# Attention on one core: the fourth product of weights and V by seven smaller ones in 21 periods instead of 6, joint VectorE operations, and instruction orders written out anew

## The chip, the cores and the metric

One core of a Trainium2 chip runs the whole kernel; seven other cores are idle. The metric is the device time of one execution in microseconds (us), median of several runs. Five engines work side by side, each through its own list of instructions in order: TensorE (PE in the profile; its weight loads are PEld), VectorE (DVE), ScalarE (ACT), GpSimd (POOL) and SyncE (SP), of which the last issues transfers only. An instruction that needs another engine's result waits on a semaphore, and everything behind it on its engine waits too.

## The reference

Softmax attention over 8 batches of 2048 rows with 512 columns, without a mask:

```python
def reference(q, k, v):                       # each (8, 2048, 512), float32
    d_k = q.shape[-1]
    scores = np.matmul(q, k.transpose(0, 2, 1)) / np.sqrt(d_k)
    attn_weights = special.softmax(scores, axis=-1).astype(np.float32)
    return np.matmul(attn_weights, v)
```

Q, K and V are rounded to float16 as they are loaded; products accumulate in float32.

## The kernel before, in words

**Seven products for eight.** A product of two matrices that are cut into 2x2 blocks takes eight products of blocks. The kernel uses a scheme with seven, numbered 1 to 7, and pays for it with sums of blocks: four sums of the left matrix's blocks, four of the right's (`s1`, `s2`, `s4`, a third that is written in place, and `t1`, `t2`, `t4`, `t3`), and additions of results. Results add up in PSUM where two products go to the same bank, and through a copy or an addition where they don't.

**Scores.** K (transposed) times Q is done in groups (`Group`, L336 on): a group makes a 256 x 1024 piece of the scores in 14 matmuls of 512 columns. After each product one instruction moves its result on: `after1` copies bank x to bank y, `after5` and `after6` copy to a scratch tile `cz`, `after7` and `after3` add to it, `after4` and `after2` take exponentials straight from the banks, and `exp_right` takes one of 1024 elements from `cz`. The exponentials are the weights, in float16, in four block tiles: `left[0]`, `left[1]` and two in `right`.

**Periods.** The work is cut into 32 periods (`NP`; four per batch, `qt` is a period's number within its batch). A period `g` does four score groups for later weights and finishes 512 rows of the output from weights that are ready: two pairs of blocks of 128 rows, `a` and `b`, each by seven products with V's blocks (`Pair.product`, L484), of which each is 8 matmuls of 256 columns.

**Inner products.** Products 1, 2 and 5 of `a` and `b` together (called x, y and z) are again a 2x2 product of blocks, and are done by seven smaller products each: `fine` (L688 on), 28 matmuls of 128 columns instead of 16 of 256 for the two. Its parts 1 to 4 are words `s1` to `s4` for x, `t` for y, `u` for z and `r` for w; w is product 4 of both. Which are done so is `INNERS`, by `qt`, and `INNERS_AT` for single periods: x, y, z nearly everywhere, w in the third period of a batch except the first (periods 6, 10, 14, 18, 22, 26). An inner product needs a copy of 256 columns from bank to bank (L733), two copies of 128 to a scratch tile `ci` (L736, L741), and two additions of 128 columns from it (L742 for a, L746 for b). `a_sums` (L663) makes its sums of weights, `vi_sums` (L271) those of V; the sums for x and y are joined in one instruction of 1024 elements where `s` is 4.

**Output.** The row sums of the weights come out as one more column of products 3 and 5. `rate` (L521) takes a reciprocal for each block, `scaled` (L493, ScalarE) scales a result out of its bank, `final` (L496, VectorE) scales and adds, and a few results are added on GpSimd (L613, which takes the second part from weights' space that is free by then) or on VectorE (L583). `store` (L506) issues each 128 x 256 piece on SP.

**What sets the order.** The lists of instructions are set by hand, not by a scheduler (`manual_schedule`). Each period has 28 slots, one for each score product in a fixed order (`QORDER`), plus 6. Tables say after which slot each product of weights and V (`PRODUCTS`, `ENDS`), each sum (`SUMS`, `SUMS_AT`) and each load or transposition for the next batch (`PLAN`) is issued. The evictions follow their product at once. Loads go through POOL's queue, transpositions (DMA) and stores through SP's. PSUM's eight banks are five pools: `qx` two, `qy` and `qz` one each, for scores; `px` and `pz` two each, for the output. The opening (batch 0, first weights) is a list of words of its own (`OPENING`), with whole score tiles (`t40x` and the like, L311) in `qx`, after quarters (L327) with exponentials of 256 elements.

Of the kernel before, what the change touches and what calls it, by code (L numbers as in the profile page):

```python
# [12 lines left out]
def kernel(  # L13
# [7 lines left out]

# [41 lines left out]
    INNERS = ("xyz", "xyz", "xyzw", "xyz")  # L63
    INNERS_AT = {0: "", 2: "xyz", NP - 2: "xz", NP - 1: "xyz"}
    ALL = True
# [3 lines left out]
    stage = ctx.enter_context(tc.tile_pool(name="stage", bufs=2))  # L69
    ppool = ctx.enter_context(tc.tile_pool(name="ppool", bufs=2))  # L70
    spool = ctx.enter_context(tc.tile_pool(name="spool", bufs=1))
    opool = ctx.enter_context(tc.tile_pool(name="opool", bufs=8))
    czpool = ctx.enter_context(tc.tile_pool(name="czpool", bufs=2))
    ipool = ctx.enter_context(tc.tile_pool(name="ipool", bufs=1))
    psum = {}
    for name, bufs in (("qx", 2), ("qy", 1), ("qz", 1), ("px", 2), ("pz", 2)):
        psum[name] = ctx.enter_context(
            tc.tile_pool(name="ps_" + name, bufs=bufs, space=bass.MemoryType.PSUM)
        )

    def bank(name):
        name = "pz" if name == "py" else name
        t = psum[name].tile([P, 512], F32, tag=name)
        return t
# [3 lines left out]
    ident32 = ipool.tile([P, P], F32, tag="t2", name="ident32")  # L88
    ident_dram = nc.inline_tensor(np.eye(P, dtype=np.float32), name="attn_identity")
    nc.scalar.dma_start(out=ident32[:], in_=ident_dram.ap())  # L90
    ident = ipool.tile([P, P], F16, tag="t4", name="ident")

    ksum = [const.tile([P, NCH, 2, 2, P], F16, name=f"ks{n}") for n in (1, 2, 4)]
    kops = []
    for c in range(NCH):
        raw = const.tile([P, CH, ND, P], F16, name=f"kraw{c}")
        kops.append([raw] + [t[:, c] for t in ksum])
# [9 lines left out]
    if not ALL:  # L109
        ti3 = const.tile([P, NI, P], F16, name="ti3")  # L110
    ci = const.tile([P, 2, P], F32, name="ci")
    rate = const.tile([P, 8], F32, name="rate")
    rates = {
        tag: deque(rate[:, n:n + 1] for n in range(i, i + 4)) for tag, i in (("r1", 0), ("r2", 4))
    }
    ti = {}
# [9 lines left out]
    def load(what, b, c, pieces=(CH,), room=None):  # L126
        t = staged.get((what, b, c))
        if room is not None:
            t = staged[what, b, c] = room
        if t is None:  # L130
            t = staged[what, b, c] = stage.tile([P, CH, D], F16, tag="stage", name="stage")
# [14 lines left out]
    def rounded(what, n, copy):  # L146
        if not halved:
            t = stage.tile([P, CH, D], F16, tag="stage", name="halved")
            halved.update({x: t[:, i] for i, x in enumerate((w, m) for m in (2, 3) for w in "qk")})
        copy(out=halved[what, n], in_=firsts[what, n])  # L150

    def first_transpose(what, n):
# [3 lines left out]
        tr = psum["px"].tile([P, ND, P], dt, tag="px", name="tr")  # L156
        for dc in range(ND):
            nc.tensor.transpose(tr[:, dc, :], src[:, dc * P:(dc + 1) * P], with_[:])  # L158
# [17 lines left out]
    def transposed(what, c, n, w, copy):  # L176
        src = staged[what, 0, c]
        tr = psum["px"].tile([P, 2, ND, P], F16, tag="px", name="tr")
        for m in range(w):
            for dc in range(ND):  # L180
                nc.tensor.transpose(  # L181
                    tr[:, m, dc, :], src[:, n + m, dc * P:(dc + 1) * P], ident[:]
# [5 lines left out]
    def pe_transpose(what, c, n0=0, n1=CH):  # L188
        for n in range(n0, n1, 2):
            transposed(what, c, n, 2, nc.scalar.copy if n and n0 != n else nc.vector.tensor_copy)  # L190

    def k_blocks(c):
        w = kops[c][0][:].rearrange("p (j s) c r -> p j s c r", s=2)
# [8 lines left out]
    def k_sums(c):  # L202
        a11, a12, a21, a22 = k_blocks(c)
        _, s1, s2, s4 = kops[c]
# [7 lines left out]
    def t3_of(sp):  # L212
# [3 lines left out]
        t = pts[1][0][1][:].rearrange("p j q -> p (j q)")[:, 0:NT * 2 * P]  # L216
# [34 lines left out]
    def t3_inner(b, s):  # L251
        if s == 3:
            right = pts[b * NSP + 2][1]
            return right[:, 6, 0, :].rearrange("p (j c) -> p j c", j=NI)
        if s == 1 and not ALL:
            return ti3[:]
# [14 lines left out]
    def vi_sums(b, s):  # L271

        if not ti:
            for n in (2, 4):
                t = ipool.tile([P, 2, NI, P], F16, tag=f"t{n}", name=f"ti{n}")
                ti[n] = [t[:, s] for s in range(2)]
            t = ipool.tile([P, NI * (P + UP)], F16, tag="t1", name="ti1")
            ti[1] = [
                t[:, a:a + NI * w].rearrange("p (n c) -> p n c", n=NI) for a, w in ((0, P), (NI * P, UP))
            ]  # L280
            nc.gpsimd.memset(ti[1][1][:, :, P:P + 1], 0.0)
# [6 lines left out]
        else:  # L288
            b11, b12, b21, b22 = (x[:, s] for x in vi_blocks(b))
            t1, t2, t4 = (ti[n][s][:, :, 0:P] for n in (1, 2, 4))  # L290
        return [
            lambda: sub(t1, b12, b11),
            lambda: sub(t2, b22, t1),
            lambda: sub(t3_inner(b, s), b22, b12),
# [3 lines left out]
    def new_p(sp):  # L298
        left = ppool.tile([P, 2, NJ, QH], F16, tag="left", name="left")
        right = ppool.tile([P, NJ, 2, QH], F16, tag="right", name="right")  # L300
        pts[sp] = ((left[:, 0], left[:, 1]), right, left)
# [4 lines left out]
    def plain_tile(kb, half, name):  # L306
# [8 lines left out]
        left, right = pts[0][0:2]  # L315
        exp(right[:, kb // 2, kb % 2, :] if half else left[kb % 2][:, kb // 2, :], st[:])
# [3 lines left out]
    def plain_eighth(j, part, s, name="qx"):  # L320
# [11 lines left out]
        if s == 1:  # L332
            for n in range(2):
                exp(pts[0][0][n][:, j, part * w:(part + 1) * w], st[:, n * w:(n + 1) * w])

    class Group:  # L336


        def __init__(self, sp, j):
            self.sp, self.j = sp, j  # L340
            self.own = "q" if sp or j % 2 == 0 else "p"

        def product(self, n):
# [5 lines left out]
            t3 = t3_of(self.sp)  # L349
            if n == 1:  # L350
                if self.sp not in pts:
                    new_p(self.sp)
                self.left, self.right = pts[self.sp][0:2]
                self.x = bank("qx")
            elif n == 5:
                self.z = bank(self.own + "z")
            lhs, rhs, dst = {
                1: (a11, b11, "x"),
                2: (a12, b21, "y"),
                3: (s4, b22, "z"),  # L360
                4: (a22, t4, "x"),
                5: (s1, t1, "z"),
                6: (s2, t2, "x"),
                7: (a21, t3, "x"),
            }[n]
            dst = getattr(self, dst)
            for dc in range(2):
                nc.tensor.matmul(  # L368
                    dst[:], lhs[:, j, dc, :], rhs[:, :, dc, :],
# [3 lines left out]
            getattr(self, f"after{n}", lambda: None)()  # L373

        def after1(self):

            self.y = bank(self.own + "y")
            f = nc.scalar.copy if self.sp else nc.vector.tensor_copy
            f(out=self.y[:], in_=self.x[:])  # L379

        def after5(self):
            self.cz = czpool.tile([P, 2, QH], F32, tag="cz", name="cz")
            f = nc.scalar.copy if self.sp else nc.vector.tensor_copy
            f(out=self.cz[:, 1, :], in_=self.z[:])  # L384

        def after6(self):
            nc.scalar.copy(out=self.cz[:, 0, :], in_=self.x[:])  # L387

        def after7(self):
            nc.vector.tensor_add(self.cz[:, 1, :], self.x[:], self.cz[:, 1, :])  # L390

        def after3(self):
            nc.vector.tensor_add(self.cz[:, 0, :], self.z[:], self.cz[:, 0, :])  # L393

        def after4(self):
            exp(self.left[1][:, self.j, :], self.x[:])

        def after2(self):
            exp(self.left[0][:, self.j, :], self.y[:])

        def exp_right(self):
            exp(self.right[:, self.j], self.cz[:])
# [3 lines left out]
    def p_sums(g, which, j0=0, j1=NJ):  # L406

        left, right = pts[g // 2][0:2]
        if g not in psums:
            if g >= NP - 2:  # L410
# [4 lines left out]
                    [kops[c][0][:].rearrange("p n c r -> p (n c r)") for c in range(2)],  # L415
# [4 lines left out]
            else:  # L420
                psums[g] = [
                    spool.tile([P, NJ, 2 * P], F16, tag=f"s{n}", name=f"s{n}") for n in (1, 2, 4)
                ]
# [5 lines left out]
        a11, a21 = left[0][:, js, cols], right[:, js, 0, cols]  # L429
        a12, a22 = left[1][:, js, cols], right[:, js, 1, cols]  # L430
# [14 lines left out]
    spare_halves = deque()  # L445

    class Pair:

        halves = 0

        def __init__(self, g, which):
            self.g, self.which = g, which

        def product(self, n, j0=0, j1=NJ):
            g = self.g
            left, right = pts[g // 2][0:2]
            s1, s2, s4 = (t[:, :, part(self.which)] for t in psums[g])
            vh, t1, t2, t4 = vraw[g // NQT % 2], vt1, vt2, vt4  # L460
            cols = columns(g, self.which)
            alone = g >= NP - 2 and self.which == "b"
            own = "q" if alone else "p"
            if n == 1 and j0 == 0:
                self.x = bank("px")
            elif n == 2 and type(self) is Pair:
# [604 lines left out]
```

## Time and profile before

| | |
|---|---|
| three runs, us | 785.23, 785.78 (median), 786.10 |
| the profiled execution, span, us | 783.04 |
| outside the span (median less span) | 2.74 |
| TensorE busy, matmuls | 778.0 us, 99%, 6706 |
| VectorE busy, instructions | 721.2 us, 92%, 1579 |
| ScalarE busy, instructions | 648.7 us, 83%, 1375 |
| GpSimd busy, instructions | 129.4 us, 17%, 166 |

Matmuls overlap each other, so the length of one in the profile is more than the time by which it moves the next one back; the pace is read from the distance of starts. A row of the timeline gives start, length, engine, line, operation, and what goes out and in, with a count where alike instructions follow each other. In a row of a group, two numbers follow the bar: the busy time of all and the mean length of one in ns; behind the second bar stands the idle time of the engine just before them and what ended it.

### The profile page before, as it was taken

The page shows a single profiled execution, that of the slowest core. Times are in us where ns is not written, and L with a number is a line of the kernel's source. Part 1 is how long each engine was busy: PE and PEld are TensorE (multiplying, and loading weights), DVE is VectorE, ACT ScalarE, POOL GpSimd, SP SyncE. Part 2 cuts the span into 40 slices and gives each one's busy share as a digit, 9 for nine tenths or more (in the row PEclk, how much of TensorE's full clock was granted, in tenths as well). Part 3 has the DMA queues.
Part 4 walks back from the last instruction along what each step waited for, and adds up shares of the span by engine and source line. Part 5 has one row for each costly group of instructions (what it writes and reads, how often), then busy time and mean ns, then how long its engine had stood idle before and what let it go on. Part 6 is the DMA issues. An engine that isn't in the chain of part 4 may idle for free.

```text
span 783.0 us, 18335 instructions
## 1 busy us (share of the span) xinstructions
PE 778.0 (99%) x6706; PEld 538.4 (69%) x6706; DVE 721.2 (92%) x1579; ACT 648.7 (83%) x1375; POOL 129.4 (17%) x166
## 2 busy tenths in 40 slices
PE   9999999999999999999999999999999999999998
PEld 6566666676667666666766666666667666666677
DVE  3789999989999999999999999999999999999985
ACT  5687888988988888888888888888888888988873
POOL 4011211111121111211202121021210222101100
PEclk9999999999999999999999999999999999999999
DMA  9989990999919997299974999369993899911113
GB/s 225 181 146 166 191 188 33 176 181 183 195 32 197 200 175 155 59 190 190 179 139 93 187 201 189 88 126 192 185 179 83 143 189 181 203 49 42 55 56 108
DMA packets 206457, 116.07 MB, mean 148 GB/s; under 512 B 124320, under 2 KB 205344, under 8 KB 206368
## 3 DMA queue, kind: packets, MB, share of 16 engines
q0 software_dynamic: 49648, 49.29, 42.7%
q1 hardware_dynamic: 156432, 65.30, 39.9%
q8 instruction: 52, 0.85, 0.5%
q10 hardware_dynamic: 288, 0.33, 0.1%
q14 instruction: 37, 0.30, 0.1%
HBM read 100.73 MB, written 33.55 MB: 171 GB/s over the span
## 4 chain that ended last, share of the span: by engine, by line
PE 99%; ACT 0%; issue 0%; DVE 0%; ACTq 0%; DVEq 0%
PE t L368 47%; PE t L484 28%; PE t L718 20%; PE t L311 2%; PE tr L181 1%; PE t L957 1%; PE t L327 0%; PE tr L158 0%; ACT o L493 0%; ACT left L304 0%; ACT kraw L160 0%; ACT t L607 0%; DVE warm L912 0%; ACT end_ci L736 0%; DVE rate L521 0%
## 5 line engine op out<-in xcount | busy, mean ns | idle before, releaser
L368 PE MATMUL t<-qraw,kraw 128*128 128x512 f16 x728 | 198.0, 379 | 0.0
L493 ACT ACTIVATE o<-t,rate 128x256 f32<-128x256 f32 x286 | 131.0, 484 | 66.7 <-DVE rate L521 26.1
L718 PEld LDWEIGHTS <-left 128*128 128x128 f16 x2020 | 137.8, 98 | 52.8 <-DVE left L673 1.5
L304 ACT ACTIVATE left<-t 128x512 f16<-128x512 f32 (+1 forms) x260 | 155.7, 606 | 9.3 <-PE t L368 3.6
L368 PE MATMUL t<-qs,ks 128*128 128x512 f16 x488 | 140.1, 379 | 0.0
L368 PEld LDWEIGHTS <-kraw 128*128 128x128 f16 x976 | 88.0, 98 | 62.7 <-issue 0.7
L304 ACT ACTIVATE right<-cz 128x1024 f16<-128x1024 f32 x122 | 129.8, 1064 | 0.3
L484 PEld LDWEIGHTS <-s 128*128 128x128 f16 x976 | 93.9, 98 | 28.7
L484 PEld LDWEIGHTS <-right 128*128 128x128 f16 x928 | 90.5, 98 | 29.6
L393 DVE TENSOR_TENSOR cz<-t,cz 128x512 f32<-128x512 f32 x122 | 83.6, 685 | 19.5 <-ACT cz L387 12.0
L384 ACT COPY cz<-t 128x512 f32<-128x512 f32 x120 | 70.5, 587 | 25.0 <-PE t L368 23.8
L368 PEld LDWEIGHTS <-ks 128*128 128x128 f16 x732 | 66.6, 98 | 34.9 <-issue 0.3
L718 PE MATMUL t<-vh,left 128*128 128x128 f16 x964 | 83.7, 219 | 0.0
L390 DVE TENSOR_TENSOR cz<-t,cz 128x512 f32<-128x512 f32 x122 | 82.9, 679 | 0.9 <-PE t L368 0.9
L613 POOL TENSOR_TENSOR o<-o 128x256 f32<-128x256 f32 x30 | 34.3, 1144 | 237.2 <-ACT o L493 189.6
L368 PE MATMUL t<-qs,kraw 128*128 128x512 f16 x244 | 72.6, 379 | 0.0
L368 PE MATMUL t<-qraw,ks 128*128 128x512 f16 x244 | 72.6, 379 | 0.0
L379 ACT COPY t<-t 128x512 f32<-128x512 f32 x120 | 70.1, 584 | 3.0 <-PE t L368 0.9
L387 ACT COPY cz<-t 128x512 f32<-128x512 f32 x122 | 71.2, 583 | 0.6 <-PE t L368 0.3
L496 DVE SCALAR_TENSOR_TENSOR o<-t,rate,o 128x256 f32<-128x256 f32 x132 | 62.6, 477 | 7.3 <-PE t L484 5.1
L718 PE MATMUL t<-ti,left 128*128 128x128 f16 (+1 forms) x708 | 68.5, 219 | 0.0
L484 PE MATMUL t<-vt,s 128*128 128x256 f16 (+1 forms) x496 | 64.3, 273 | 0.0
(152 smaller groups left out, 1234.7 us busy)
## 6 DMA issues: line engine op xcount, KB each, us to landing
out_dram<-o SPq DMA_DIRECT2D x256, 128.0 KB, 2.6
vh<-in_v_dram POOLq DMA_DIRECT2D x32, 512.0 KB, 10.6
stage<-in_q_dram POOLq DMA_DIRECT2D x28, 512.0 KB, 7.4
stage<-in_k_dram POOLq DMA_DIRECT2D x28, 512.0 KB, 8.0
right<-in_q_dram POOLq DMA_DIRECT2D x2, 512.0 KB, 10.0
right<-in_k_dram POOLq DMA_DIRECT2D x2, 512.0 KB, 12.4
first<-in_q_dram SPq DMA_DIRECT2D x2, 256.0 KB, 3.5
cz<-in_q_dram SPq DMA_DIRECT2D x2, 256.0 KB, 5.2
```

Source lines behind the costliest of these rows:

```text
L304: nc.scalar.activation(out=out_, in_=in_, func=EXP, scale=inv_sqrt_d)
L368: nc.tensor.matmul(dst[:], lhs[:, j, dc, :], rhs[:, :, dc, :], start=(n in (1, 5) and dc == 0), stop=(dc == 1), skip_group_check=True,)
L379: f(out=self.y[:], in_=self.x[:])
L384: f(out=self.cz[:, 1, :], in_=self.z[:])
L387: nc.scalar.copy(out=self.cz[:, 0, :], in_=self.x[:])
L390: nc.vector.tensor_add(self.cz[:, 1, :], self.x[:], self.cz[:, 1, :])
L393: nc.vector.tensor_add(self.cz[:, 0, :], self.z[:], self.cz[:, 0, :])
L484: nc.tensor.matmul(dst[:, 0:width], lhs(j), rhs(j), start=(first and j == 0), stop=(j == NJ - 1), skip_group_check=True,)
L493: nc.scalar.activation(out=out_, in_=src, func=COPY, scale=r)
L496: nc.vector.scalar_tensor_tensor(out=out_, in0=src, scalar=r, in1=out_, op0=MULT, op1=ADD)
L613: nc.gpsimd.tensor_add(self.o11, self.o11, more)
L718: nc.tensor.matmul(dst, lhs[:, j, :], rhs[:, j, :], start=(n == 1 and j == 0), stop=(j == NI - 1), skip_group_check=True,)
```

## The change

```diff
-    INNERS = ("xyz", "xyz", "xyzw", "xyz")
-    INNERS_AT = {0: "", 2: "xyz", NP - 2: "xz", NP - 1: "xyz"}
+    INNERS = ("xyz", "xyzw", "xyzw", "xyzw")
+    INNERS_AT = {0: "", NP - 3: "xyz", NP - 2: "xz", NP - 1: "xyz"}
...
+    banks = ppsum.tile([P, 8, 512], F32, tag="banks", name="banks")
+    homes = {"qx": deque((0, 1)), "qy": deque((2,)), "qz": deque((3,)),
+             "px": deque((4, 5)), "pz": deque((6, 7))}
+
+    def spot(name):
+        turns = homes["pz" if name == "py" else name]
+        turns.rotate(-1)
+        return turns[-1]
...
-    def k_sums(c):
-        a11, a12, a21, a22 = k_blocks(c)
-        _, s1, s2, s4 = kops[c]
+    def k_sums(c, n=1):
+        a11, a12, a21, a22 = k_blocks(c, n)
+        s1, s2, s4 = (t[:, c:c + n].rearrange("p n j c r -> p (n j) c r") for t in ksum)
...
+    outs = [const.tile([P, 2, H], F32, name=f"o{n}") for n in range(4)]
+    ptiles = [const.tile([P, 4, NJ, QH], F16, name=f"left{n}") for n in range(2)]
...
+    def joint_rate(g, tag):
+        low = pair_of(g, "z")[0]
+        n = (0 if tag == "r1" else 4) + g % 2 * 2
+        nc.vector.reciprocal(out=rate[:, n:n + 2], in_=banks[:, low:low + 2, H])
...
+        elif x in "DP":
+            o = room_of(g, w, "o22")
+            (nc.vector if x == "D" else nc.gpsimd).tensor_add(o, o, room_of(g, w, "o21"))
+            store(g, w, "o22")
+        elif x in "MV":
+            name, n, tag = ("w", 1, "r2") if x == "M" else ("y", 0, "r1")
+            scaled(second_half(g, w, n), in_two(side(g, w, name)[:, 0:H]), rate_of(g, w, tag))
+        elif x in "NW":
+            to, n = ("o21", 1) if x == "N" else ("o11", 0)
+            o = in_two(room_of(g, w, to))
+            nc.gpsimd.tensor_add(o, o, second_half(g, w, n))
+            store(g, w, to)
...
+            n = int("w" not in INNER(g))
+            t = pts[g // 2][:, n:3]
+            a11, a12, a21, a22 = (t[:, :, j, c] for c in (ca, cb) for j in (lo, hi))
...
+        elif what == "+":
+            both = banks[:, low:low + 2, P:H]
+            nc.vector.tensor_add(both, both, cs[:])
...
-            nc.vector.tensor_add(xa[:, P:H], xa[:, P:H], cs[:, 0])
...
-            nc.vector.tensor_add(xb[:, P:H], xb[:, P:H], cs[:, 1])
...
     for g in range(NP):
-        todo = after_slot(g)
-        work = placed(SUMS_AT[g] if g in SUMS_AT else SUMS[g % NQT])
...
+        order = ORDERS.get(g, ORDERS[f"row {g % NQT}"])
+        for word in order.split():
+            emit(g, word)
```

In words:

- **w in 21 periods:** the second, third and fourth period of the first seven batches. `a_sums` with `s` 4 sums the weights of x, y and w in one instruction of 1536 elements there; in the second and fourth periods the last of the four sums takes x and y in one and w by itself.
- **One PSUM tile** (`banks`) in place of five pools; `spot` gives the banks of a name in strict turn. The weights are two fixed tiles of four blocks, the outputs four fixed tiles, the scratch tiles two.
- **Joint operations:** the word `+` adds over both banks of an inner product (2 x 128 columns) from the whole of `ci`; `R1` and `R2` take the reciprocals of `a` and `b` in one instruction; `K0` and `K1` sum K over two chunks, 1024 elements, beside the old `k` words.
- **Output additions:** words `P` (o22 and o21), `N` and `W` (a result and its second half, kept in weights' space) are on GpSimd.
- **Orders:** for each of the first four and last three periods, and for each `qt` otherwise, one list of words takes the place of the slot tables. A digit and a point with a group's number (`1.0`) is a score product; `y`, `c`, `d`, `e`, `f`, `l`, `h`, `r` with a number are the instructions that move a group's results on, now words of their own, and so are the copies (`sc`, `sd`, `se`), the additions (`s+`) and the evictions (`Ea`, `Ob`, ...). A stroke (') means the period before; `<` is a transposition, `>` a load. The last period's list ends in `... Oa Oa' t4 Ib Ub b4 Ob Ua`; `b4` is the last product, `O`, `I` and `U` scale or merge a result and store it. Before, the last entries were `a4@25 b4@27`.
- The words of the opening are the same.

**ScalarE, in an ordinary period.** Names: `t` is a bank before, `banks` the one PSUM tile; `left` and `right` are weights, `left_101` and `left_102` the two fixed weight tiles; `cz_94` and `cz_95` the scratch tiles; `ci` the inner product's scratch. Before:

```order
L493 ACTIVATE o<-t,rate 128x256
L736 COPY ci<-t 128x128
L304 ACTIVATE right<-cz 128x1024
L387 COPY cz<-t 128x512
L733 COPY t<-t 128x256
L304 ACTIVATE left<-t 128x512
L741 COPY ci<-t 128x128
```

Now, in the first period of a batch:

```order
L348 COPY cz_95<-banks 128x512
L460 ACTIVATE left_102<-banks,rate 128x2x128
L630 COPY ci<-banks 128x128
L350 COPY cz_95<-banks 128x512
L279 ACTIVATE left_102<-cz_94 128x2x512
L628 COPY banks<-banks 128x256
L279 ACTIVATE left_102<-banks 128x512
L632 COPY ci<-banks 128x128
```

The exponential from `cz` moved behind the copy to the other `cz`, so it stands directly ahead of the inner product's copy and the exponential of 512. The eviction of 2x128 is one whose result goes to weights' space.

**VectorE, in an ordinary period.** `s_...` are sums of weights, `ti`, `vt` and `vh` V and its sums, `rate` the reciprocals. Before:

```order
L742 TENSOR_TENSOR t<-t,ci 128x128
L521 RECIPROCAL rate<-t 128x1
L393 TENSOR_TENSOR cz<-t,cz 128x512
L675 TENSOR_TENSOR left<-left 128x512
L435 TENSOR_TENSOR s_3169<-left,s_3168 128x2048
L746 TENSOR_TENSOR t<-t,ci 128x128
```

Now:

```order
L354 TENSOR_TENSOR cz_95<-banks,cz_95 128x512
L635 TENSOR_TENSOR banks<-banks,ci 128x2x128
L483 RECIPROCAL rate<-banks 128x2
L394 TENSOR_TENSOR s_100<-left_101,s_99 128x2048
L393 TENSOR_TENSOR left_101<-left_101 128x2x256
L270 TENSOR_TENSOR ti_65<-vh_77,ti_64 128x512
```

The two additions from `ci`, with three instructions and a reciprocal between them, became one over 2x128, followed by one reciprocal of two columns.

**POOL, between the loads of a batch.** `o` are output tiles, `o_90` to `o_93` the four fixed ones (o22, o12, o11, o21); the loads are `DMA` rows. Before:

```order
L613 TENSOR_TENSOR o<-o,right 128x256 x2
L135 DMA stage<-in_k_dram 128x4x512
L232 DMA vh_109<-in_v_dram 128x4x512
L135 DMA stage<-in_k_dram 128x4x512
L613 TENSOR_TENSOR o<-o 128x256 x2
L135 DMA stage<-in_q_dram 128x4x512
```

Now:

```order
L515 TENSOR_TENSOR o_92<-o_92,left_101 128x256
L507 TENSOR_TENSOR o_90<-o_90,o_93 128x256
L515 TENSOR_TENSOR o_92<-o_92,left_101 128x256
L119 DMA stage_96<-in_q_dram 128x4x512
L515 TENSOR_TENSOR o_93<-o_93,left_101 128x256
L215 DMA vh_78<-in_v_dram 128x4x512
L515 TENSOR_TENSOR o_93<-o_93,left_101 128x256
L215 DMA vh_78<-in_v_dram 128x4x512
```

Where a load stood behind two additions, additions of three kinds now stand between and among the loads: 106 in all, of which 34 are L507 and 72 L515, where 58 stood before.

More of the change, by code (lines that the diff above doesn't have):

```diff
@@ L186, in transposed, with k_blocks @@
             staged.pop((what, 0, c))
[L188 to L193, printed above, removed]
+    def k_blocks(c, n=1):
+        w = kraw[:, c * CH:(c + n) * CH].rearrange("p (j s) c r -> p j s c r", s=2)
         return w[:, :, 0, 0:2], w[:, :, 0, 2:4], w[:, :, 1, 0:2], w[:, :, 1, 2:4]
@@ L252, in t3_inner @@
         if s == 3:
[L253 to L256, printed above, removed]
+            return vw_blocks()[1]
         if b + 1 == B:
```

746 lines of the change are left out of this document (309 added, 437 removed), and 103 rows, old and new, of tables (OPENING, ORDERS, PLAN, SUMS).

## The prediction

> **What bounds the kernel now.** I read the page first, its busy times and the chain of waits:
>
> ```profile
> span 783.0 us, 18335 instructions
> PE 778.0 (99%) x6706; PEld 538.4 (69%) x6706; DVE 721.2 (92%) x1579; ACT 648.7 (83%) x1375; POOL 129.4 (17%) x166
> PE 99%; ACT 0%; issue 0%; DVE 0%; ACTq 0%; DVEq 0%
> ```
>
> TensorE has work for 99% of the span, and the chain that ended last is TensorE at 99%. Next come TensorE's waits, by engine and line waited for (total, times, longest):
>
> ```profile
> PE t L957 <- DVE warm L912: 1.2, 1, 1.2
> PE t L327 <- ACT kraw L160: 0.2, 1, 0.2
> ```
>
> Both lie in the opening; no wait for another engine is named after that. So the time is the number of matmuls by their pace. The pace is in TensorE's timeline (start, length, operation, count), in a stretch of ordinary periods and in one of the six periods with an inner product of V's fourth part:
>
> ```profile
> 252.91 1.91 PE L484 MATMUL t<-vh,right 128*128 128x256 f16 x16
> 254.65 1.03 PE L368 MATMUL t<-qs,ks 128*128 128x512 f16 x4
> 255.51 0.59 PE L368 MATMUL t<-qs,kraw 128*128 128x512 f16 x2
> ...
> 208.94 0.39 PE L718 MATMUL t<-vt,right 128*128 128x128 f16 x4
> 209.17 0.39 PE L718 MATMUL t<-wi,right 128*128 128x128 f16 x4
> 209.39 0.39 PE L718 MATMUL t<-vt,s 128*128 128x128 f16 x4
> ```
>
> The start of the next row ends the count. Sixteen matmuls of 256 columns pass from 252.91 to 254.65, 109 ns each; four of 512 from 254.65 to 255.51, 215 ns; eight of 128 from 208.94 to 209.39, 56 ns. These three prices make the main term. The last view is the sum over a batch from the middle (us from:to, length, then busy time and count of each engine, granted clock, DMA share):
>
> ```profile
> core 0: us, PE busy (x) PEld busy (x) DVE busy (x) ACT busy (x) POOL busy (x), PEclk, DMA share, GB/s
> 175.00:270.00 95.00, 95.00 (x830) 65.73 (x829) 91.31 (x201) 81.84 (x176) 17.01 (x20) 1.00 0.93 160
> ```
>
> TensorE is busy for all 95 us at full granted clock; VectorE has 3.7 us to spare, ScalarE 13.2. VectorE is therefore the engine to watch.
>
> **The products.** The fourth product of a pair of blocks is 16 matmuls of 256 columns: 16 x 109 = 1744 ns. The seven inner ones are 28 of 128 columns: 28 x 56 = 1568 ns. The difference is 176 ns a period. Before, 6 periods had this (6, 10, ..., 26); now 21 have it (the last three of each of the first seven batches), 15 more: 15 x 0.176 = **-2.64 us**. No other matmul changes: the order has 420 more of 128 columns and 240 fewer of 256.
>
> **What it costs the other engines.** Their prices, by group and tile shape (busy us, mean ns | idle before):
>
> ```profile
> L742 DVE TENSOR_TENSOR t<-t,ci 128x128 f32<-128x128 f32 x93 | 27.1, 291 | 0.8 <-PE t L718 0.2
> L393 DVE TENSOR_TENSOR cz<-t,cz 128x512 f32<-128x512 f32 x122 | 83.6, 685 | 19.5 <-ACT cz L387 12.0 <-PE t L368 7.4
> L521 DVE RECIPROCAL rate<-t 128x1 f32<-128x1 f32 x128 | 20.9, 164 | 7.6 <-PE t L484 5.4
> L496 DVE SCALAR_TENSOR_TENSOR o<-t,rate,o 128x256 f32<-128x256 f32 x132 | 62.6, 477 | 7.3 <-PE t L484 5.1 <-issue 1.4
> L583 DVE TENSOR_TENSOR o<-o 128x256 f32<-128x256 f32 x12 | 4.9, 411 | 0.0
> L674 DVE TENSOR_TENSOR s<-s 128x512 f16<-128x512 f16 x29 | 12.1, 416 | 0.0
> L672 DVE TENSOR_TENSOR left<-left 128x1024 f16<-128x1024 f16 x22 | 15.0, 682 | 0.0
> L432 DVE TENSOR_TENSOR s<-right 128x1536 f16<-128x1536 f16 x14 | 13.3, 949 | 0.0
> L736 ACT COPY ci<-t 128x128 f32<-128x128 f32 x93 | 25.2, 271 | 1.6 <-PE t L718 1.6
> L733 ACT COPY t<-t 128x256 f32<-128x256 f32 x67 | 26.2, 391 | 0.6
> L493 ACT ACTIVATE o<-t,rate 128x256 f32<-128x256 f32 x286 | 131.0, 484 | 66.7 <-DVE rate L521 26.1 <-PE t L484 16.8 <-DVE t L742 12.7
> ```
>
> VectorE: 196 additions of 128 columns from the scratch tile become 113 over two banks. No row has 256 columns; 291 and 685 ns for 128 and 512 put it between 291 (nothing for more columns) and 582 (twice one), and on their line at 0.42 us, which I take: 196 x 0.291 - 113 x 0.42 = -9.5 us (bounds -24 to +9). Reciprocals 128 to 66, a second column taken as free: -62 x 0.164 = -10.2. Scaled merges 132 to 125: -7 x 0.477 = -3.3. Additions of two results 12 to 1: -11 x 0.411 = -4.5. K sums: 72 of 512 become 36 of 1024: -30.0 + 24.6 = -5.4. Weight sums: 88 of 1024 and 24 of 512 become 70 of 1536, 18 of 1024 and 14 of 512: 78.7 + 5.8 - 60.0 - 10.0 = +14.5. V sums for one more batch: 4 x 0.416 = +1.7. Together **-16.7 us**, two per batch.
>
> ScalarE: 30 scratch copies (8.1), 15 bank copies (5.9) and 14 evictions (6.8) more: **+20.8 us**, some 3 of the 13.2 to spare in a batch. Neither engine becomes the bound, and I cost both at nothing on the path while TensorE's queued products cover them; without that cover it would be the 20.8.
>
> That is the sum over a batch; each product waits for one instruction. The thinnest place that I find is in the order of ScalarE shown ahead: exponential over both halves of a scratch tile, copy of 256, exponential of 512, before the next group's second product.
>
> ```profile
> L304 ACT ACTIVATE right<-cz 128x1024 f16<-128x1024 f32 x122 | 129.8, 1064 | 0.3
> L304 ACT ACTIVATE left<-t 128x512 f16<-128x512 f32 x252 | 153.3, 612 | 7.4 <-PE t L368 3.6 <-PE t L311 2.3
> ```
>
> These are 1.06 + 0.39 + 0.61 = 2.06 us. TensorE has, from the end of the inner product ahead of the copy, three score products (0.43 each) and two inner ones (0.22 each): 1.73 us. The exponential must start 0.33 us before the inner product ends, or TensorE waits. What is late after it is the score group's next copy, so one slip returns in the next group.
>
> K sums over two chunks need both transposed:
>
> ```profile
> kraw<-stage SPq DMA_TRANSPOSE x28, 7.2
> ```
>
> Between the second chunk's transposition and its first joint sum stand 8.9 us of TensorE work by the prices above, 1.7 more than the median landing: nothing, though later landings would hold up VectorE by the difference. The transpositions and stores stay on SP, the loads on POOL now stand behind more output additions.
>
> **POOL and VectorE.** GpSimd has 58 output additions; now 106. What one does to VectorE (timelines of VectorE and POOL, then the groups, min/median/max ns):
>
> ```profile
> 205.36 0.75 DVE L672 TENSOR_TENSOR left<-s 128x512 f16<-128x512 f16 x1
> 206.03 0.68 DVE L390 TENSOR_TENSOR cz<-t,cz 128x512 f32<-128x512 f32 x1
> ...
> 204.95 0.88 POOL L613 TENSOR_TENSOR o<-o,right 128x256 f32<-128x256 f32 x1 [2.73 <-issue]
> 206.05 0.72 POOL L613 TENSOR_TENSOR o<-o,right 128x256 f32<-128x256 f32 x1 [0.22 <-ACT right L493]
> ...
> L672 DVE TENSOR_TENSOR left<-s x29: 408/424/1173, 63.4 to 727.7; 128x512 f16<-128x512 f16 x29
> ```
>
> The sum that starts under an addition takes 0.75 us instead of 0.42 and ends just after it; the one with PSUM as an input keeps its 0.68 under the next addition. Going through the timeline I find 21 such hits, 5.0 us together, the longest the group's 1173: 0.086 us per addition. [...]
>
> The 48 more additions bring 48 x 0.086 = 4.1 us of late VectorE work at that rate, at most 48 x 0.75 = 36 us and at least none. How much reaches TensorE? In the trace, none of the 5.0 did. I take **+0.3 us**, near that end, since VectorE gains two us per batch.
>
> **Opening, small gaps, tail.** The banks now turn strictly. The first whole score tile waited for the second of six exponentials; by the new turn it waits for the fourth (PE; ScalarE from its second and from its fourth):
>
> ```profile
> 13.90 1.02 PE L311 MATMUL t<-qraw,kraw 128*128 128x512 f16 x4
> ...
> 13.47 0.65 ACT L304 ACTIVATE left<-t 128x256 f16<-128x256 f32 x2
> 14.00 0.96 ACT L304 ACTIVATE left<-t 128x256 f16<-128x256 f32 x3
> ```
>
> Two take 0.65 and start 0.27 apart, so one takes 0.38: the second ends at 13.85, the fourth at 14.4: **+0.5 us**, between 0 (the order hides it) and 0.9 (each later tile slips too).
>
> ```profile
> 69.48 0.59 PE L368 MATMUL t<-qs,ks 128*128 128x512 f16 x2
> 70.09 0.59 PE L368 MATMUL t<-qs,kraw 128*128 128x512 f16 x2
> ```
>
> Two of 512 fill 0.43 of the 0.61 us from 69.48. It is the last of three such gaps of 0.17 us; the others are near 42 and 56. The order there is new: **-0.5 us** if all go, 0 if none. I take them as gone, since a single copy of 0.27 us (the L736 group) that stands earlier makes up for 0.17; A has the case that they come back.
>
> ```profile
> 779.57 0.47 ACT L493 ACTIVATE o<-t,rate 128x256 f32<-128x256 f32 x1 [0.40 <-PE t L484]
> L506 SPq DMA_DIRECT2D out_dram<-o x256: 332/333/2062, 52.4 to 780.1; - x128
> ```
>
> The list of the last period now ends in the last product, its eviction with its store, and the merge and store of one result more; that store stands behind the eviction's on SP, one issue (0.333 us) later: **+0.35 us** (0 to 0.7).
>
> **Sum.** The profiled execution has a span of 783.04 us, the three runs a median of 785.78, 2.74 more; I make the sum on the median. 785.78 - 2.64 + 0.5 - 0.5 + 0.35 + 0.3 = **783.8 us** (a span near 781.05). The bounds of the small terms give 782.6 to 784.2 for this case, taken so that not all fall on one side.
>
> **Rivals.** *A, the gain is handed back.* If the thin ScalarE place opens a gap of 0.17 us, like those above, in every second of 28 periods: 14 x 0.17 = 2.4 us, 783.5 + 2.4 = 785.9, no change. For it: 0.33 us must be ahead at each of them, and ScalarE has 3 us per batch more. Against it: in the trace such gaps stop at 70 us, with VectorE as full.
>
> *B, slower: the output additions lock VectorE where sums feed products.* All of the 4.1 us of new lateness reaches TensorE, and a third of the old 5.0, since margins are used up: 5.8 us, 783.5 + 5.8 = 789.3. It decides from 3.9 us on (783.5 + 3.9 = 787.4). The place is the weight sums of the periods with four inner products, three-wide now. For it: 106 additions, and sums that are longer. Against it: the copies of K, V and weights are summed some periods ahead, and VectorE has 5.7 us to spare per batch instead of 3.7.
>
> *C, the pace of 56 ns is not held,* so that the change doesn't do what it says:
>
> ```profile
> L718 PEld LDWEIGHTS <-left 128*128 128x128 f16 x2020 | 137.8, 98 | 52.8 <-DVE left L673 1.5 <-DVE left L675 1.3
> ```
>
> A weight load takes 98 ns; were it not hidden, each of the new 420 would cost 42 ns more: 17.6 us, 801.1. Against it: the rows from 208.94 on are this very product at 56.
>
> **Chances.** Forecast 0.57, A 0.25, B 0.15, C 0.03. What a measurement of this kernel can tell from no change is about 0.2%, 1.57 us: below 784.21 is faster, above 787.35 slower. So faster 0.57, same 0.25 (A), slower 0.18 (B and C). The range, 782.6 to 788.0, holds the forecast, A and the lower part of B.
>
> **What would show it.** Right: TensorE 99% of the chain again, matmuls of 128 columns at 56 ns and 420 more, VectorE near 704 us busy, ScalarE near 669, the joint addition near 0.42 us, no wait of TensorE past 80 us. The opening: the first score tile at 14.4 instead of 13.9. A shows as many gaps of TensorE of some 0.2 us behind ScalarE's exponentials; B as weight sums well over their 0.95 and 0.68 us, with TensorE waiting for VectorE; C as 128-column matmuls 98 ns apart. I'm wrong if the joint additions take 0.58 us, or if the new order has waits of a kind that the old one never showed.

## The result and the profile after

| | before | after |
|---|---|---|
| median of six runs, us | 785.5 | 812.62 (808.42 to 821.06) |
| profiled execution, span, us | 783.04 | 813.30 |
| TensorE busy, matmuls | 778.0 us, 6706 | 785.3 us, 6886 |
| VectorE busy, instructions | 721.2 us, 1579 | 732.0 us, 1374 |
| ScalarE busy, instructions | 648.7 us, 1375 | 668.3 us, 1434 |

The ratio is 1.034 (1.031 to 1.037): slower by 27 us, well above the range. (Here and below medians are of all runs, while ratios leave disturbed runs out; the two differ slightly for three kernels.) The page of the change, busy times and chain of waits:

```profile
span 813.3 us, 18359 instructions
PE 785.3 (97%) x6886; PEld 540.9 (67%) x6886; DVE 732.0 (90%) x1374; ACT 668.3 (82%) x1434; POOL 162.4 (20%) x214
PE 79%; DVE 10%; DMA 8%; issue 1%; ACT 1%; POOL 0%; ACTq 0%; DVEq 0%; POOLq 0%
```

TensorE, 99% of the chain before, is 79% now; VectorE and DMA have the rest. Waits of the change, first the three largest of TensorE, then two of ScalarE and VectorE from the whole list (total us, times, longest):

```profile
PE banks L454 <- ACT o L460: 14.9, 10, 3.4
PE banks L645 <- ACT o L460: 3.2, 1, 3.2
PE banks L335 <- DVE cz L354: 1.2, 4, 0.4
...
ACT o L460 <- DMA out_dram<-o: 13.3, 5, 4.4
DVE ks L189 <- DMA kraw<-stage: 12.8, 5, 3.8
```

TensorE waits for evictions (L460, formerly L493), which before it never did past the opening. Behind that stand two waits that no row of before had at all: an eviction that waits for an earlier store out of its output tile, and a joint sum of K (L189) that waits for a transposition. Before, neither engine waited for a transfer after the opening.

One batch shows how both arise. Timelines of POOL, SP, ScalarE, VectorE and TensorE in the change (start, length, engine, line, operation, count; in brackets the idle time before, and what ended it):

```profile
140.49 0.72 POOL L507 TENSOR_TENSOR o<-o,o 128x256 f32<-128x256 f32 x1 [12.04 <-ACT o L460]
141.47 0.72 POOL L507 TENSOR_TENSOR o<-o,o 128x256 f32<-128x256 f32 x1 [0.26 <-ACT o L460]
142.14 0.78 POOL L119 DMA_DIRECT2D stage<-in_q_dram  x1
...
166.99 0.74 POOL L119 DMA_DIRECT2D stage<-in_k_dram  x1 [12.55 <-DMA qraw<-stage]
...
151.11 5.87 SPq L158 DMA_TRANSPOSE qraw<-stage  x1
...
169.63 6.12 SPq L158 DMA_TRANSPOSE kraw<-stage  x1
175.84 1.50 SPq L469 DMA_DIRECT2D out_dram<-o  x3
177.45 3.70 SPq L158 DMA_TRANSPOSE kraw<-stage  x1
...
181.01 0.47 ACT L460 ACTIVATE o<-banks,rate 128x256 f32<-128x256 f32 x1 [4.40 <-DMA out_dram<-o]
187.54 0.84 ACT L460 ACTIVATE o<-banks,rate 128x256 f32<-128x256 f32 x2 [3.60 <-DVE rate L483]
...
186.73 0.69 DVE L189 TENSOR_TENSOR ks<-kraw 128x1024 f16<-128x1024 f16 x1 [3.77 <-DMA kraw<-stage]
187.34 0.16 DVE L483 RECIPROCAL rate<-banks 128x2 f32<-128x2 f32 x1
...
181.54 3.60 PE L454 MATMUL banks<-vh,s 128*128 128x257 f16 x16 [3.37 <-ACT o L460]
184.93 0.63 PE L645 MATMUL banks<-ti,left 128*128 128x128 f16 x4
```

POOL stands 12 us behind output additions that wait for ScalarE, and Q's second load, issued at 142.14, stands behind them. Its transposition is issued at 151.11; only when that has landed is the staging tile free for K's second load (12.55 us of waiting, 166.99). That load's transposition is issued at 177.45, and the joint sum gets it at 186.73. VectorE waits 3.77 us for it, with the reciprocals queued behind (187.34); ScalarE's eviction waits for those (3.60). On the other side K's first transposition holds SP for 6.12 us from 169.63, stores stand behind it, and ScalarE, whose next result goes to an output tile not yet stored, waits 4.40 us. TensorE stops for 3.37 us at 178. Then it runs slow (window from:to, length, busy time and count of each engine, granted clock):

```profile
181.54:184.93 3.39, 3.39 (x16) 2.36 (x16) 0.43 (x1) 2.40 (x5) 0.00 (x0) 0.50 1.17 200
```

Sixteen matmuls take 3.39 us instead of 1.75, at a granted clock of 0.50 (the last section lists the gaps behind which that came).

The 30.3 us between the spans, worked out from the distances of starts in TensorE's timeline: matmuls at their price -2.6; opening +0.65; small gaps before 80 us -0.5; waits for stores 9.3; waits for the K sum 9.7; half clock behind three gaps 5.9; VectorE late elsewhere 6; tail 1.4; end of the last period 0.5.

### The profile page after: what moved, and what is told of

Same layout as the page of the kernel before. It is cut to its first block, busy times and chain, and to the rows that moved or that the text cites. A ratio compares the mean times of both kernels' runs of the same rounds, so it can differ in the third digit from the quotient of the medians.

```text
span 813.3 us, 18359 instructions
## 1 busy us (share of the span) xinstructions
PE 785.3 (97%) x6886; PEld 540.9 (67%) x6886; DVE 732.0 (90%) x1374; ACT 668.3 (82%) x1434; POOL 162.4 (20%) x214
## 4 chain that ended last, share of the span: by engine, by line
PE 79%; DVE 10%; DMA 8%; issue 1%; ACT 1%; POOL 0%; ACTq 0%; DVEq 0%; POOLq 0%
PE banks L335 37%; PE banks L454 20%; PE banks L645 19%; DMA kraw<-stage 6%; PE banks L286 2%; DMA out_dram<-o 1%; DVE cz L352 1%; DVE left L595 1%; DVE left L597 1%; DVE s L392 1%; DVE left L594 1%; DVE left L393 1%; DVE cz L354 1%; DVE left L596 1%; DVE o L463 1%
## 5 line engine op out<-in xcount | busy, mean ns | idle before, releaser
L645 PEld LDWEIGHTS <-left 128*128 128x128 f16 x2608 | 177.7, 98 | 75.9 <-issue 3.5
L335 PE MATMUL banks<-qraw,kraw 128*128 128x512 f16 x728 | 203.8, 380 | 0.0
L279 ACT ACTIVATE left<-banks 128x512 f16<-128x512 f32 (+1 forms) x272 | 160.8, 602 | 20.3 <-PE banks L335 11.4
L335 PE MATMUL banks<-qs,ks 128*128 128x512 f16 x488 | 143.8, 382 | 1.3 <-DVE cz L354 1.2
L460 ACT ACTIVATE o<-banks,rate 128x256 f32<-128x256 f32 x248 | 114.3, 481 | 37.4 <-DVE rate L483 15.0
L279 ACT ACTIVATE left<-cz 128x1024 f16<-128x1024 f32 x122 | 129.8, 1064 | 3.7 <-DVE cz L354 3.2
L515 POOL TENSOR_TENSOR o<-o,left 128x256 f32<-128x256 f32 x72 | 65.8, 921 | 259.1 <-ACT left L460 207.0
L354 DVE TENSOR_TENSOR cz<-banks,cz 128x512 f32<-128x512 f32 x122 | 83.6, 685 | 10.3 <-PE banks L335 4.6
L645 PE MATMUL banks<-vh,left 128*128 128x128 f16 x964 | 87.9, 219 | 0.7
L352 DVE TENSOR_TENSOR cz<-banks,cz 128x512 f32<-128x512 f32 x122 | 83.5, 684 | 5.5 <-PE banks L335 5.2
L350 ACT COPY cz<-banks 128x512 f32<-128x512 f32 x122 | 72.7, 596 | 16.0 <-PE banks L335 16.0
L454 PEld LDWEIGHTS <-left 128*128 128x128 f16 x736 | 71.1, 98 | 19.4 <-ACT left L460 0.6
L348 ACT COPY cz<-banks 128x512 f32<-128x512 f32 x120 | 71.0, 591 | 8.2 <-PE banks L335 6.4
L335 PE MATMUL banks<-qraw,ks 128*128 128x512 f16 x244 | 72.7, 380 | 0.0
```

The lines of the kernel that those rows point to most:

```text
L279: nc.scalar.activation(out=out_, in_=in_, func=EXP, scale=inv_sqrt_d)
L335: nc.tensor.matmul(dst, lhs[:, j, dc, :], rhs[:, :, dc, :], start=(n in (1, 5) and dc == 0), stop=(dc == 1), skip_group_check=True,)
L348: self.copy(out=cz[:, 0, :], in_=self.z)
L350: nc.scalar.copy(out=cz[:, 1, :], in_=self.x)
L352: add(cz[:, 0, :], self.x, cz[:, 0, :])
L354: add(cz[:, 1, :], self.z, cz[:, 1, :])
```

## The experiments

The columns "store" and "transposition" give the longest waits of ScalarE for a store and of VectorE for a transposition of K (total us, times). Ratios are against runs of before beside each kernel.

| kernel | us | ratio | store | transposition |
|---|---|---|---|---|
| change | 812.62 | 1.034 (1.031 to 1.037) | 13.3, 5 | 12.8, 5 |
| transfers back, first try | 798.0 | 1.016 (1.013 to 1.019) | 2.4, 1 | none |
| transfers back, mended | 793.76 | 1.012 (1.009 to 1.016) | 2.7, 3 | none |
| loads alone back | 808.12 | 1.029 (1.024 to 1.034) | none | 14.4, 4 |
| K's transpositions alone back | 816.08 | 1.035 (1.030 to 1.041) | 20.2, 7 | none |
| one load earlier | 805.23 | 1.025 (1.022 to 1.027) | 9.0, 6 | 6.3, 3 |
| K sums split | 806.54 | 1.026 (1.021 to 1.032) | 20.4, 10 | none |
| two merges in place of four words | 813.31 | 1.039 (1.032 to 1.045) | 9.8, 2 | 8.2, 4 |
| these three | 799.73 | 1.018 (1.016 to 1.020) | 3.3, 2 | none |
| no output additions | 788.98 | 1.005 (1.003 to 1.008) | 2.1, 1 | 1.4, 2 |
| transfers back, no output additions | 787.09 | 1.002 (1.001 to 1.003) | 0.2, 1 | none |
| transfers back, w merged | 806.84 | 1.028 (1.026 to 1.030) | 1.8, 3 | none |
| transfers back, end and one load moved | 791.35 | 1.008 (1.006 to 1.009) | 1.9, 1 | none |

**Transfers back at their old places.** The lists hold most loads and transpositions later than the old slots did. By the last score product that stands ahead (counted from 0, 28 to a period), old and new: first period of a batch `>q1` 5 and 14, `<q1` 16 and 17, `>v0` 14 and 21, `>k0` 18 and 22, `>k1` 24 and 26; second `<k0` 0 and 5, `<k1` 5 and 12, `>k2` 8 and 15, `<k2` 20 and 22, `>k3` 16 and 20; third `>q2` 0 and 17, `<k3` 5 and 12. Two stand earlier in these lists (`<q0` 10 and 9, `>v3` 20 and 18), and in the first batch more do; so not all are later by 0 to 17, as the expectation has it. The edit moves all loads and transpositions back and leaves all else; four of its places:

```diff
-  4.p v02 r.p u1 3.0 d.0 r5'
+  4.p v02 r.p u1 3.0 >q1 d.0 r5'
...
-  f.1 u3 >q1 h.1 1.2
+  f.1 u3 h.1 1.2
...
-  e.p 1.0 a7' y.0 4.p 5.0 2.0 6.0 l.p d.0 v14 1.1 <k0 S2
+  e.p 1.0 <k0 a7' y.0 4.p 5.0 2.0 6.0 l.p d.0 v14 1.1 <k1 S2
...
-  3.1 R2 <k1 Ob'
+  3.1 R2 Ob'
```

> The changed kernel with only the loads and transpositions put back at the score products after which they stood before (all of them later by 0 to 17 products in the change). Theory D (transfers issued too late and on top of each other, so that K sums wait for transpositions and evictions wait for stores behind them on SP): the waits of ScalarE for stores (9.3 us of TensorE's gaps in the profile of the change), of VectorE for the K transpositions (9.7) and the half clock after them (5.6) go, 812.6 - 24.6 = 788. Rival J (joined K sums and output tiles with fixed names are what waits, wherever the transfers stand): over 800. Rival L (GpSimd's additions lock VectorE): over 808, since they stay.

It gained 14.6 us. In period 1 it also put a transposition of K ahead of the last product that reads the old chunk, so that product reads other data; TensorE waited 4 us there. With `<k1` behind `4.p` in that period:

> As the first of these runs, but in the second period of batch 0 the transposition of K's second chunk stands behind the last product that reads the old chunk. There it stood ahead of it, which made that product wait for the new chunk (4.2 us, and 2.7 at half clock after it) and read other data. Theory D: 798 - 7 = 791. What is left over the 785.4 of before would be gaps of 0.1 to 1.6 us with no transfer behind them.

793.76: 18.9 of the 27 us go when only the places of these words change. Its waits of TensorE show what is left:

```profile
PE banks L335 <- DVE cz L354: 2.0, 5, 0.7
PE banks L824 <- DVE ti L783: 1.2, 1, 1.2
PE banks L645 <- DVE banks L635: 1.0, 3, 0.4
PE banks L286 <- ACT left L279: 0.4, 1, 0.4
PE banks L454 <- ACT o L460: 0.3, 1, 0.3
```

What waits there are is for VectorE (`cz`, `ti`, `banks`); those for evictions went from 18.1 us to 0.3. One batch (us from:to, length, busy time and count of each engine, clock, DMA share), first mended, then in the change:

```profile
175.00:270.00 95.00, 94.33 (x846) 65.02 (x845) 91.52 (x170) 83.69 (x182) 20.00 (x27) 1.00 0.87 153
```

```profile
175.00:270.00 95.00, 90.72 (x788) 61.80 (x787) 84.72 (x154) 77.99 (x169) 20.97 (x27) 0.96 0.88 148
```

TensorE lacks 0.67 us in place of 4.28, at the full clock.

**Which of the words.** Only the loads (`>`) back, and only K's transpositions with `<q1` back:

> The changed kernel with only the loads (POOL) put back, the transpositions (SP) where the change has them. If late loads are the start of it (theory Q): as with both put back, 792 to 797. If a load that runs under a transposition is what makes the transposition long (rival C): the loads now start under the late transpositions as the earlier single load showed, 800 to 808.

> The changed kernel with only K's four transpositions and the second of Q put back in the periods from the second batch on, the loads where the change has them. Theory Q: they wait on SP for loads that are late, and hold the stores behind them longer, 810 or more. Rival C: they get out of the way of the next loads, below 805.

Each removes one wait and leaves or raises the other: with the loads alone back no eviction waits for a store, but the K sum waits 14.4 us; with the transpositions alone back it is 20.2 us of waits for stores. Neither half gives much; together they give 18.9 us. One load of the change, moved ahead of the additions that it stood behind (two in the timeline above, not the four of the expectation):

```diff
-  e.p 6.0 Pa' c.0
+  e.p 6.0 >q1 Pa' c.0
...
-  f.1 u3 >q1 h.1 1.2
+  f.1 u3 h.1 1.2
```

> The changed kernel with one word moved: in the first period of each batch but the first, the load of the second part of Q stands ahead of GpSimd's first output addition there instead of behind four of them. Theory Q (that load waits behind additions that wait for ScalarE, and through the two staging tiles it makes the four loads and transpositions after it late): 812.6 less the part of the 19 us that putting all of them back gave, 795 to 800. Rival P (each load and transposition is late by its own place in the order): over 808.

A gain of 7.4 us: the load was issued at 126.0 instead of 142.1, but its transposition, still at its late place under the loads of V and K (148.12 and 148.90), held up the next load of K until 161.48, and POOL stood idle for 11.83 us before that.

**K sums split, merges, and all three.** First the joint sums of the second period taken apart again:

```diff
-  s4 r.1 K01 1.3
+  s4 r.1 k01 1.3
...
-  q1 K03 Ha
+  q1 k11 k03 k13 Ha
...
-  Wa K04 f.3
+  Wa k04 k14 f.3
```

> The changed kernel with the joint sums of K's first two chunks undone: the first chunk's sum stands where the joint one stood, the second chunk's three words later in the same period. Theory D and rival J alike: the 9.7 us of waits for the K transpositions go and with them a half clock of 1.5, so about 801; waits for stores stay. Rival L: no change, 810 to 815.

The wait for the transposition went and that for stores rose from 13.3 to 20.4 us: my reading, not tried by itself, is that evictions came on time again and ran into stores that had not landed. Second, in the first period of a batch the last products are merged on VectorE, not scaled and added on GpSimd (`Va`, `Vb` dropped, `Wa`, `Wb` made `Ua`, `Ub`), which frees a place on POOL ahead of a load:

> The changed kernel with the first result of each first period of a batch merged on VectorE from the bank (one scaled merge of 0.48 us) instead of evicted by ScalarE and added on GpSimd. Theory D: only the gaps that follow VectorE's long weight sums under these additions go, some 3.5 us: about 809, with the waits for transfers as before. Rival L: all of VectorE's lateness starts there, below 800.

No gain. Third, both of these with the first try of the transfers:

> The three edits together. Theory D: 788 less 3.5, about 784 to 785, as before the change or a little under. Rivals J and L together: the same. Over 790 would mean that something else is late too.

It equals the transfers alone and repeats their fault in period 1; the other two edits add nothing.

**Output additions.** All 106 on GpSimd left out (so the outputs lack what they add), with the transfers back, and in the order of the change:

```diff
-            (nc.vector if x == "D" else nc.gpsimd).tensor_add(o, o, room_of(g, w, "o21"))
+            if x == "D":
+                nc.vector.tensor_add(o, o, room_of(g, w, "o21"))
...
-            nc.gpsimd.tensor_add(o, o, second_half(g, w, n))
```

> The run before this one, with all 106 output additions on GpSimd left out (so those outputs lack their second part; stores stay). Theory L2 (what is left after the transfers are put back is VectorE held up by these additions): 784 to 786. Rival T (the written order is too tight for ScalarE's and VectorE's own times): no change, about 791.

> The changed kernel with the same 106 additions left out and the loads and transpositions as the change has them. If the additions only hold up VectorE: 812.6 less about 6, 804 to 809. If they are also what makes the loads late, by standing ahead of them on GpSimd's queue (rival Q): below 798, with the waits for K transpositions and stores gone.

| us | words late | words back |
|---|---|---|
| with additions | 812.6 | 793.8 |
| without | 789.0 | 787.1 |

Late words cost 18.9 us with the additions and 1.9 without; the additions cost 23.6 us under late words and 6.7 otherwise. Some 17 us belong to the two together. By the timeline above I take this to be POOL's queue: an addition that waits for ScalarE holds the loads behind it, and the late words leave no time for that; the gain from the load moved ahead of them agrees with it. Since a store waits for its addition too, the runs don't tell the part of the loads from that of the stores. The other 6.7 us, with the words back, are TensorE waiting for VectorE: by the distances of its starts past 80 us, TensorE loses some 7 us behind VectorE and in small gaps with the additions, and under 1 us without. One such place: VectorE, POOL and TensorE with the words back, then VectorE at the same place without additions:

```profile
582.86 2.54 DVE L393 TENSOR_TENSOR left<-left 128x2048 f16<-128x2048 f16 x1
582.89 1.42 POOL L515 TENSOR_TENSOR o<-o,left 128x256 f32<-128x256 f32 x2
586.06 0.59 PE L335 MATMUL banks<-qs,ks 128*128 128x512 f16 x2 [0.68 <-DVE cz L354]
```

```profile
578.34 1.22 DVE L393 TENSOR_TENSOR left<-left 128x2048 f16<-128x2048 f16 x1
```

The sum beside two additions takes 2.54 us in place of 1.22, the addition to `cz` (L354) stands behind it on VectorE, and TensorE waits 0.68 us for that. All of VectorE's instructions together last 825.3 us with the additions and 811.3 without. Which sums are hit changes with the order. First the change, then the kernel with the words back, in which the hits have moved to other sums (busy us, mean ns), then the last group without additions:

```profile
L595 DVE TENSOR_TENSOR left<-left,left 128x1536 f16<-128x1536 f16 x7 | 9.6, 1373 | 0.0
L597 DVE TENSOR_TENSOR left<-left,left 128x1536 f16<-128x1536 f16 x7 | 9.2, 1307 | 0.2
```

```profile
L595 DVE TENSOR_TENSOR left<-left,left 128x1536 f16<-128x1536 f16 x7 | 6.6, 945 | 0.0
L597 DVE TENSOR_TENSOR left<-left,left 128x1536 f16<-128x1536 f16 x7 | 6.7, 957 | 0.2
L391 DVE TENSOR_TENSOR s<-left 128x2048 f16<-128x2048 f16 x15 | 21.5, 1434 | 0.0
```

```profile
L391 DVE TENSOR_TENSOR s<-left 128x2048 f16<-128x2048 f16 x15 | 18.2, 1210 | 0.0
```

The window of the same batch without additions, words back:

```profile
175.00:270.00 95.00, 95.00 (x858) 66.01 (x856) 90.65 (x172) 84.74 (x185) 8.88 (x12) 1.00 0.89 159
```

There TensorE is busy for all of the 95 us. Could VectorE do the work instead? With the transfers back, `M` and `N` of w (scale, add) became `T`, VectorE's merge; in one period of four an addition then reads a result that already holds the fourth product, so that this output differs:

> The first of these four with the 36 additions of the fourth product's second half taken from GpSimd: VectorE merges the result from its bank (0.48 us), and ScalarE's 36 evictions of it go. Theory L2: half of what the additions cost comes back, about 788. Rival V (VectorE has no room): over 793.

13 us worse: with VectorE at 742.4 us busy, TensorE has work for 93.19 us of 95 in each of the two batches from 175 us on, and of the 14.5 us that its waits list, 10.5 are for VectorE. For these 36, GpSimd's additions are the cheaper way.

**The best of these.** Transfers back, `>q1` ahead of `Pa'`, and at the end one eviction moved up and the last merge ahead of the last product:

```diff
-  s+ t3 R1 b4' Ga
+  s+ t3 R1 Oa' b4' Ga
...
-  t2 a7 b7 Ia a4 Oa Oa' t4 Ib Ub b4 Ob Ua
+  t2 a7 b7 Ia a4 Oa t4 Ib Ub Ua b4 Ob
```

> All loads and transpositions put back, and the end of the last period's list changed: one eviction moved up to where its product ends, and the last merge ahead of the last product, so that one store instead of five is still to be issued when that product ends. If the end is set by SP's issues one behind the other, 0.9 us less than the 793.8 of the run without it, and the span behind the last matmul 4.0 us instead of 5.2.

791.35, 2.4 us better than without these two edits, and the best with all of the work in it; before is still faster by 0.75% (0.6 to 0.9). Which of the two edits gave it stays open: in its profiled run the last seven store issues lie between 782.33 and 788.62 on SP, 6.29 us, where the last eight of the kernel without these edits took 5.42, and that hides the end.

## Why the prediction was wrong, point by point

- **The step that failed** is the one on the loads and transpositions: "1.7 more than the median landing: nothing", and "the loads on POOL now stand behind more output additions" with no price. It compared one landing with the work behind its issue and took the issue's place for granted. The first of these is also counted wrong: between `<k1` and the first joint sum `K01` the list has 8 score products, 7 inner and 2 plain ones, 6.7 us by the forecast's prices, which is less than the median landing of 7.2; 8.9 us reach to the later `k02`. Above all the forecast did not follow the words: what the load waits for on POOL, when the staging tile is then free, what the transposition holds up on SP, and that an eviction into one of four fixed output tiles waits for that tile's last store. The words' places cost 18.9 us, 17 of them only together with the output additions. The median landing was 6.6 us before and 8.5 us in the change.
- **The main term held:** 420 matmuls of 128 columns more, 240 of 256 fewer, at the old prices where the clock is full (56, 109 and 215 ns by the distances of starts from 106.32 to 109.38); -2.6 us is in the accounting. Rival C did not occur.
- **VectorE was mis-sized:** 704 us forecast, 732.0 measured. Counted as in the forecast, against the lengths in the kernels without additions, 38 instructions beside GpSimd's additions were longer, by 15.1 us together, where before it was 21 by 5.0: 0.14 us per addition and not 0.086, 10 us more in place of 4.1. Apart from that the lengths sum to 12.1 us less (forecast 16.7). But instructions were priced by their length. VectorE starts the next before the last has ended:

```profile
203.75 0.95 DVE L594 TENSOR_TENSOR left<-left 128x1536 f16<-128x1536 f16 x1
204.61 0.43 DVE L635 TENSOR_TENSOR banks<-banks,ci 128x256 f32<-128x256 f32 x1
204.95 0.68 DVE L352 TENSOR_TENSOR cz<-banks,cz 128x512 f32<-128x512 f32 x1
205.54 1.44 DVE L595 TENSOR_TENSOR left<-left,left 128x1536 f16<-128x1536 f16 x1
```

  The 0.95 us from 203.75 move the next start by 0.86, the 0.43 by 0.34. With 205 fewer instructions there are fewer such overlaps, of some 82 ns each: together they fell from 108.2 to 95.4 us, which takes back the 12.1. So joining, with the longer weight sums, gave VectorE nothing, and the two spare us per batch that were to cover these hits did not exist. The joint addition at 429 ns was forecast at 0.42.
- **ScalarE** held: 669 forecast, 668.3. Rival A's thin place made no gaps; the time was lost elsewhere.
- **Rival B** named the right place of loss at 0.15: VectorE's sums longer beside additions (2.54 us in place of 1.22 above), with TensorE waiting behind (0.68). Its place holds in part. In the change the three-wide sums are late (1.37 us in place of 0.95), but TensorE then waits only 0.11 us in each of six batches; with the words back other sums are late, and TensorE waits behind those. By the runs the additions cost 6.7 us with the words back (B gave 5.8), a quarter of the loss; the forecast itself had 0.3 us for it.
- **Opening:** the first whole score tile started at 14.55, forecast 14.4; +0.65 us, forecast +0.5. **Small gaps:** gone, as forecast. **Tail:** +1.4 us, forecast +0.35. The last five stores are all issued after the last matmul has started (808.14), one behind the other, the last at 810.24: the five issues took SP from 808.27 to 810.64, and the forecast had counted one, of 0.33 us.
- The text named its own fault at its end, "waits of a kind that the old one never showed", without giving it a price or a chance.

## What to carry to other kernels

When an order is rewritten, follow each transfer's word through its queue as carefully as the instructions: what waits ahead of it, which buffer it frees and who needs that next. POOL's queue carried both waiting arithmetic and loads here, and a shift of words became a chain of waits (12.04 us on POOL, then 3.77 on VectorE); its price, 18.9 us with the additions, was 1.9 without them, so try both corners of such a pair. Price instructions by the distance of their starts, not by their length, before counting on a gain from joining them.

## What the runs showed of the hardware

- Transpositions that land late go with loads in flight: in the change, from 60 to 700 us, a median of 5.05 us with none at any time on the way, 7.2 with one and 10.3 with two or more. A slow one also meets more loads; counted by the loads in flight at its issue, the medians are 5.7, 8.6 and 10.9 us in the change, but 6.4, 5.9 and 8.4 before. The issue of one holds SP for long (K's, min/median/max ns, then all transpositions from issue to landing):

```profile
L158 SPq DMA_TRANSPOSE kraw<-stage x28: 1779/5255/7852, 61.5 to 689.7; - x28
DMA to landing us min/median/max: 4.3/8.5/18.8
```

- Half clock came in the change behind three idle times of TensorE, of 3.22, 3.37 and 2.82 us (ended at 114.94, 181.54 and 678.53): the granted clock is 0.50 from 115.33 to 118.73, from 181.54 to 186.99 and from 678.54 to 681.92. Behind 2.67, 1.87 and 1.20 us (ended at 482.06, 286.86 and 380.28) it is 1.00 in the 3.4 us that follow. What decides between the two is not shown. By the distances of starts, a stretch at half clock cost the change 1.6 to 2.7 us beside the gap.
- Times scatter more in the change: 808.42 to 821.06 over six runs, where before had 785.09 to 786.52. That its waits for transfers cause this is not shown.
